# Scores of a neighbourhood-attention mixer: two stacked products over 128 rows, or three split products over 64 rows with two heads on the two halves of the array

## The chip, the core and the metric

The kernel runs on one core of a Trainium2 chip. A core has a matrix engine (TensorE, "PE" in the profile, with its weight loads listed apart as "PEld"), VectorE ("DVE"), ScalarE ("ACT"), GpSimd ("POOL") and a queue engine (SyncE, "SP") that mostly issues DMAs. A matmul keeps one operand in the array (the stationary one, loaded beforehand), streams the other past it, and adds up over the array's rows, which are partitions of on-chip memory. Results go to banks of a separate memory, PSUM, 128 partitions by 512 floats each. The metric is the time of one execution on the device in microseconds; lower is better.

## What is computed

A bidirectional encoder of two layers over 512 tokens of width 1024, in float32. Each layer is a half feed-forward step, a token mixer, a cross-attention into 256 memory tokens and another half feed-forward step, each followed by a layer norm. The change is in the mixer of the odd layer (there is one): neighbourhood attention on a grid of 8 rows by 64 columns, 16 heads of width 64. Each token attends to all 8 rows and 16 neighbouring columns, with a learned bias.

```python
def mixer_c(h, w_in, w_out, rpb):
    q, k, v = jnp.split(h @ w_in, 3, axis=-1)
    ...
    def row_block(r):
        ...
        bias = rpb[:, dr[None, :, None] + NA_KH - 1, dc[:, None, :] + NA_KW - 1]
        s = jnp.einsum('bwhd,bawjhd->bhwaj', q_r, k_nb).astype(jnp.float32) * scale
        s = s + bias.astype(jnp.float32)[None]
        p = jax.nn.softmax(s.reshape(B, C_HEADS, GRID_W, kh * kw), axis=-1)
        p = p.reshape(B, C_HEADS, GRID_W, kh, kw).astype(v.dtype)
        return jnp.einsum('bhwaj,bawjhd->bwhd', p, v_nb)
    ...
    return o @ w_out
```

## The kernel before

Everything is kept transposed where TensorE needs it: features on partitions, 512 tokens along the free axis. To get float32 results from a one-pass format ("fp32r"), each operand is split into a high part and the rest: `split` (L364) rounds on ScalarE and subtracts on VectorE. A product of two split operands is three matmuls: high by high, high by low, low by high (`mm3`, L375).

`mixer_c` (L1247) works on eight pairs of heads. One pair's queries are a 128 by 512 product: the first head's 64 features are on partitions 0 to 63, the second head's on 64 to 127; the same holds for the keys. `queries` (L1270) and `keys` (L1286) project them into a PSUM bank and split them into two small tiles ("t2", 128x512). They then copy halves of these between partitions by DMA on SP's queue. A head's query tile gets its 64 high rows on top and its 64 low rows below; its two key tiles hold the high rows twice and the low rows twice. One matmul over 128 rows then gives (high + low) of the query by one part of the key, and two matmuls give all four products. That takes 4 copies for queries and 8 for keys of each pair, 128 KB each. In the profile they are "slab<-t" on SP's queue.

`weights_of` (L1323) makes the scores. The 64 grid columns are taken in four column blocks (`C_BLOCKS`, L36): 128 queries (16 columns of 8 rows) against 24, 32, 32 and 24 columns of keys, which is 192, 256, 256 and 192 keys. For each of the two heads, one after the other, and each block: two matmuls into a PSUM bank of tag "a"; VectorE adds the bias, writes the sum to a t2 tile and takes the minimum (the scores are negated); ScalarE takes the exponential with its sum. After a head's four blocks, a reciprocal on VectorE and four normalisations on ScalarE follow.

`turned` (L1353) then transposes the weights on TensorE and splits them; `attend` (L1366) multiplies them with the values into two banks of tag "d". `values` (L1253) projects values, `share` (L1386) and `down` (L538) the output.

Nothing is issued in the order in which it is written. All calls go to `Graph.record` (L138). `Graph.plan` (L182) runs a simple model of the engines over the recorded operations, with costs from `Graph.cost` (L113), and fixes each engine's order. On TensorE the ready operation that was recorded first goes first; on VectorE, ScalarE and GpSimd a second pass orders by due time. Buffers of a tag are granted in the order of recording as they come free: 14 for "t2", 27 for "slab" (128x1024), and for PSUM banks 3 for "a", 2 for "d" and 3 for "t" (`BUFS`, L341). The loop of `mixer_c` (L1401) records for each pair: the next pair's keys, the transposes of this pair's weights, the queries after next, the next pair's `weights_of`, this pair's `attend`, then values. Every operation is called from one helper, so the profile puts nearly all of them on L157, and they are told apart by their tiles.

Of the kernel before, what the change touches and what calls it, by code (L numbers as in the profile page):

```python
# [12 lines left out]
F32 = mybir.dt.float32  # L13
# [3 lines left out]
AF = mybir.ActivationFunctionType  # L17
ALU = mybir.AluOpType
AX = mybir.AxisListType

P = 128
# [7 lines left out]
ROWS = S // GRID_W  # L29
# [6 lines left out]
C_BLOCKS = [(0, 24, 0), (8, 32, 1), (24, 32, 1), (40, 24, 2)]  # L36
# [29 lines left out]
class Graph:  # L66
# [45 lines left out]
    @staticmethod  # L112
    def cost(engine, method, out, ins, kw):  # L113
        n = 1
        for d in (out if method != "tensor_reduce" else ins[0]).ap[1:]:
            n *= d[1]
        wide = any(z.space == bass.MemoryType.PSUM for z in ins + [out]) if engine != "sync" else False
        if method == "dma_start":
            return 1200.0 if "accum_op" in kw else 600.0
        if engine == "tensor":  # L120
            return max(n / 2.4 + 14, 111)
        scalars = sum(1 for z in ins if z.ap[-1][1] == 1)
        aside = 120.0 * any(Graph.extent(z)[0] > 0 for z in ins + [out])
        if engine == "vector":
            if method == "tensor_scalar" and not wide:
                n = n / 2
            return n / 0.96 + 72 + aside + 60 * scalars + 120 * (method == "scalar_tensor_tensor" and "accum_out" in kw)
        if engine == "scalar":
            scaled = 42 * hasattr(kw.get("scale"), "tensor")
            return n / 1.2 + (55 if wide else 100) + aside + 45 * scalars + 130 * ("accum_out" in kw) + scaled  # L130
        if n <= 8:
            return 270.0 if method == "tensor_scalar" else 200.0 if method != "tensor_tensor" else 390.0 + 157.0 * n
        if method == "memset":
            return n * 0.83 + 60
        dense = len(ins) == 2 and all(z.ap[-1][0] != 0 for z in ins)
        return n * (2.4 if dense else 1.7) + (70 if dense else 130)
# [184 lines left out]
class Kernel:  # L321
# [925 lines left out]
    def mixer_c(self, ln_i, last):  # L1247
        nc, a = self.nc, self.a
# [21 lines left out]
        def queries(pair, first=False):  # L1270

            if pair % 2 == 0:
                wq[0] = self.w_cols(w_in, 128 * pair)
            ps = self.ps("a" if first else "d")
            for lo, hi in [(0, 128), (128, 256), (256, 512)] if first else [(0, 512)]:
                self.project(wq[0][pair % 2], ps, lo, hi)
            parts = self.t2(), self.t2()
            self.split(ps, *parts, scale=-0.125)
            qs[pair] = self.pair()
            for s, z in enumerate(qs[pair]):  # L1280
                for i, part in enumerate(parts):
                    nc.sync.dma_start(
                        out=z[64 * i : 64 * i + 64].bitcast(F32), in_=part[64 * s : 64 * s + 64].bitcast(F32)
                    )

        def keys(pair, first=False):  # L1286

            if pair % 2 == 0:
                wk[0] = self.w_cols(w_in, D + 128 * pair)
            ps = self.ps("a" if first else "t")  # L1290
            for lo, hi in [(0, 256), (256, 512)] if first else [(0, 512)]:
                self.project(wk[0][pair % 2], ps, lo, hi)
            parts = self.t2(), self.t2()
            self.split(ps, *parts)
            ks[pair] = [self.pair() for _ in range(2)]
            for s, both in enumerate(ks[pair]):
                for z, part in zip(both, parts):
                    for i in range(2):
                        nc.sync.dma_start(
                        out=z[64 * i : 64 * i + 64].bitcast(F32), in_=part[64 * s : 64 * s + 64].bitcast(F32)  # L1300
                    )

        def biases(pair):

            table, inner = self.t2(F32), self.t2(F32)
            got = []
            for s in range(2):
                tab = table[:, s * 256 : s * 256 + 256]
                nc.gpsimd.dma_start(out=tab, in_=self.bias[2 * pair + s])
                outer = self.t2(F32)  # L1310
                dst = [outer[:, 0:192], inner[:, s * 256 : s * 256 + 256], outer[:, 192:384]]
                for i, off in enumerate((64, 0, 0)):
                    n = dst[i].shape[1]
                    nc.gpsimd.tensor_tensor(
                        out=dst[i].rearrange("p (u r) -> p u r", r=8),
                        in0=self.near[:, i, : n // 8].rearrange("p (u o) -> p u o", o=1).broadcast_to([P, n // 8, 8]),
                        in1=tab[:, off : off + n].rearrange("p (u r) -> p u r", r=8),
                        op=ALU.subtract,
                    )
                got.append(dst)  # L1320
            return got

        def weights_of(pair):  # L1323

            got = []
            for q, k, table in zip(qs.pop(pair), ks.pop(pair), biases(pair)):
                both = [self.t2(F32), self.t2(F32)]
                nc.gpsimd.memset(both[0][:, 0:64], 0.0)
                nc.gpsimd.memset(both[1][:, 448:512], 0.0)
                l = self.small(4, "l4")  # L1330
                us = []
                for t, (kc, w, kind) in enumerate(C_BLOCKS):
                    n = w * ROWS
                    ps = self.ps("a")
                    for i in range(2):
                        nc.tensor.matmul(
                            ps[:, :n], q[:, t * P : (t + 1) * P], k[i][:, kc * 8 : kc * 8 + n], start=i == 0, stop=i == 1
                        )
                    c0 = (t % 2) * 256 + (64 if t == 0 else 0)
                    u = both[t // 2][:, c0 : c0 + n]  # L1340
                    mn = self.small(1, "mn")
                    nc.vector.tensor_tensor_reduce(
                        out=u, in0=ps[:, :n], in1=table[kind], scale=1.0, scalar=3e38, op0=ALU.add, op1=ALU.min, accum_out=mn,
                    )
                    nc.scalar.activation(u, u, AF.Exp, bias=mn, scale=-1.0, accum_out=l[:, t : t + 1])
                    us.append(u)
                nc.vector.reciprocal(l, l)
                for t, u in enumerate(us):
                    self.normalise(u, l[:, t : t + 1])
                got.append([z[:, c * 256 : c * 256 + 256] for z in both for c in range(2)])  # L1350
            return got

        def turned(us):  # L1353

# [38 lines left out]
        vp, qs, ks, acts = {}, {}, {}, []  # L1393
        wv, wq, wk, wo = [None], [None], [None], {}
        for t in range(NT):
            values(0, t)
        queries(0, True)
        keys(0, True)
        queries(1)
        us = weights_of(0)  # L1400
        for pair in range(8):  # L1401


            if pair < 7:
                keys(pair + 1)
            else:
                for n in range(3, 5):
                    share(n)
            pts = turned(us)
            if pair < 6:  # L1410
                queries(pair + 2)
            else:
                for n in (0, 1) if pair == 6 else (5, 6, 7):
                    share(n)
            if pair < 7:
                us = weights_of(pair + 1)
            acts.append(attend(pts, pair))
            if pair == 6:
                self.memory_tokens()
            if pair < 6:  # L1420
                for t in range(2):
                    values(pair // 2 + 1, 2 * (pair % 2) + t)
            elif pair == 6:
                share(2)
# [241 lines left out]
```

## Time and profile before

| | |
|---|---|
| time of the kernel, median of 3 runs | 2128.33 us (2128.21 to 2129.47) |
| span of the profiled execution, first to last instruction | 2123.9 us |
| that execution's own whole time | not given; the median lies 4.4 us above the span |
| mean granted TensorE clock | 0.998 |

The profile is of one execution. Times in its lines are microseconds unless marked ns. "a<-slab,slab" reads: written to a tile of tag a, from tiles of tag slab. "128*128 128x256" on a matmul is 128 array rows by 128 columns with an output of 128 partitions by 256. A windows line gives a stretch, its length, then for PE, PEld, DVE, ACT and POOL the busy time with the number of instructions, the granted clock, the share of time of the DMA engines and GB/s. Matmuls are pipelined and the ends in their records are modelled, so the time from one start to the next tells what a matmul takes, not its length.

### The profile page before, as it was taken

The page shows a single profiled execution, that of the slowest core. Times are in us where ns is not written, and L with a number is a line of the kernel's source. Part 1 is how long each engine was busy: PE and PEld are TensorE (multiplying, and loading weights), DVE is VectorE, ACT ScalarE, POOL GpSimd, SP SyncE. Part 2 cuts the span into 40 slices and gives each one's busy share as a digit, 9 for nine tenths or more (in the row PEclk, how much of TensorE's full clock was granted, in tenths as well). Part 3 has the DMA queues.
Part 4 walks back from the last instruction along what each step waited for, and adds up shares of the span by engine and source line. Part 5 has one row for each costly group of instructions (what it writes and reads, how often), then busy time and mean ns, then how long its engine had stood idle before and what let it go on. Part 6 is the DMA issues. An engine that isn't in the chain of part 4 may idle for free.

```text
span 2123.9 us, 32745 instructions
## 1 busy us (share of the span) xinstructions
PE 2109.2 (99%) x12648; PEld 1871.0 (88%) x12648; DVE 1735.8 (82%) x2500; ACT 1161.2 (55%) x1903; POOL 287.4 (14%) x379
## 2 busy tenths in 40 slices
PE   9999999999999999999999999999999999999997
PEld 7999988888888899998889999888888888999996
DVE  7789988888748879998879999866577479699997
ACT  5555443698546554545545455457764465444552
POOL 0001015310102000000200000312210021000003
PEclk9999999999999999999999999999999999999999
DMA  6566562004434346564445556356454433456551
GB/s 205 141 168 144 136 191 91 21 18 116 140 125 109 90 117 181 150 158 129 148 100 143 126 139 186 78 147 165 119 165 155 139 93 96 110 149 155 143 149 60
DMA packets 208860, 275.93 MB, mean 130 GB/s; under 512 B 10688, under 2 KB 151616, under 8 KB 208704
## 3 DMA queue, kind: packets, MB, share of 16 engines
q1 hardware_dynamic: 175904, 221.14, 34.0%
q0 software_dynamic: 32512, 52.44, 14.1%
q8 instruction: 100, 1.64, 0.3%
q14 instruction: 56, 0.46, 0.1%
q10 hardware_dynamic: 288, 0.26, 0.0%
HBM read 259.12 MB, written 4.19 MB: 124 GB/s over the span
## 4 chain that ended last, share of the span: by engine, by line
PE 96%; DVE 1%; ACT 1%; DMA 1%; issue 0%; SPq 0%; DVEq 0%; ACTq 0%
PE a L157 59%; PE d L157 23%; PE t L157 15%; DVE slab L157 1%; ACT t L157 1%; DMA slab<-t 1%; DVE x L157 0%; ACT slab L157 0%; SPq L157 0%; DVE t L157 0%; DMA raw<-x_t 0%; ACT xh L157 0%; DVE mn L157 0%; DVE xl L157 0%; DVEq L1662 0%
## 5 line engine op out<-in xcount | busy, mean ns | idle before, releaser
L157 DVE TENSOR_TENSOR slab<-slab,slab 128x1024 fp32r<-128x1024 f32 (+3 forms) x638 | 727.5, 1166 | 69.5 <-ACT slab L157 39.9
L157 ACT CAST slab<-slab 128x1024 fp32r<-128x1024 f32 (+2 forms) x498 | 472.7, 983 | 341.5 <-DVE slab L157 173.2
L157 PE MATMUL a<-slab,slab 128*128 128x256 f32 (+3 forms) x2320 | 567.2, 322 | 0.7 <-DMA slab<-t 0.4
L157 PE MATMUL a<-xh,slab 128*128 128x256 f32 (+2 forms) x2480 | 559.9, 315 | 0.3 <-ACT slab L157 0.3
L157 PE MATMUL d<-slab,slab 128*128 128x512 f32 (+2 forms) x1856 | 447.0, 381 | 0.0
L157 PEld LDWEIGHTS a<-xh,slab 128*128 128x128 f32 x2480 | 416.4, 190 | 33.7 <-ACT slab L157 1.0
L157 PEld LDWEIGHTS a<-slab,slab 128*128 128x128 f32 x2320 | 409.5, 190 | 38.8 <-ACT t L157 1.3
L157 PE MATMUL a<-xl,slab 128*128 128x256 f32 (+1 forms) x1240 | 389.7, 314 | 0.0
L157 PE MATMUL a<-raw,slab 128*128 128x256 f32 x2048 | 388.9, 283 | 0.1
L157 PEld LDWEIGHTS d<-slab,slab 128*128 128x128 f32 x1856 | 329.0, 189 | 55.9 <-issue 0.2
L157 PEld LDWEIGHTS a<-raw,slab 128*128 128x128 f32 x2048 | 327.9, 192 | 5.4 <-ACT slab L157 0.5
L157 PEld LDWEIGHTS a<-xl,slab 128*128 128x128 f32 x1240 | 236.0, 190 | 18.4 <-DVE xl L157 0.4
L157 PE MATMUL t<-slab,slab 128*128 128x512 f32 (+1 forms) x840 | 209.5, 389 | 0.0
L157 DVE TENSOR_TENSOR slab<-raw,slab 128x1024 fp32r<-128x1024 f32 (+2 forms) x140 | 160.2, 1160 | 18.6 <-ACT slab L157 18.4
L157 PEld LDWEIGHTS t<-slab,slab 128*128 128x128 f32 x840 | 149.9, 189 | 26.3
L157 DVE TENSOR_TENSOR slab<-t,slab 128x512 fp32r<-128x512 f32 (+2 forms) x223 | 137.6, 638 | 16.4 <-ACT slab L157 15.9
L157 ACT CAST slab<-t 128x512 fp32r<-128x512 f32 (+2 forms) x223 | 120.9, 566 | 40.7 <-DVE t L157 13.9
L157 ACT CAST slab<-raw 128x1024 fp32r<-128x1024 f32 (+1 forms) x132 | 124.3, 971 | 27.9 <-PE a L157 8.8
L157 DVE SCALAR_TENSOR_TENSOR x<-d,x 128x512 f32<-128x512 f32 x168 | 114.7, 685 | 25.3 <-PE d L157 24.4
L157 ACT COPY t<-a 128x512 f32<-128x512 f32 (+1 forms) x116 | 63.5, 550 | 130.4 <-PE a L157 77.2
L157 POOL DMA_DIRECT2D slab<-ffn_w_down x40 | 47.7, 1193 | 310.3 <-DVE slab L157 276.3
L157 ACT ACTIVATE t<-a 128x512 f32<-128x512 f32 (+3 forms) x65 | 36.3, 559 | 89.0 <-PE a L157 89.0
(126 smaller groups left out, 2167.2 us busy)
## 6 DMA issues: line engine op xcount, KB each, us to landing
slab<-ffn_w_gate SPq DMA_DIRECT2D x80, 512.0 KB
slab<-ffn_w_up SPq DMA_DIRECT2D x80, 512.0 KB
slab<-ffn_w_down SPq DMA_DIRECT2D x80, 512.0 KB
slab<-ffn_w_down POOLq DMA_DIRECT2D x40, 512.0 KB, 5.8
raw<-mem_w_kv SPq DMA_DIRECT2D x16, 1024.0 KB
slab<-t SPq DMA_DIRECT2D x96, 128.0 KB
slab<-ffn_w_gate POOLq DMA_DIRECT2D x16, 512.0 KB, 7.8
slab<-ffn_w_up POOLq DMA_DIRECT2D x16, 512.0 KB, 6.0
```

What stands on the lines that cost most here:

```text
L157: op.call = lambda: fn(*args, **kw)
```

## The change

- The copies between partitions are gone. `queries` and `keys` split the projected bank straight into one pair of slabs (`split_t2`, L948: ScalarE writes the high part, VectorE the rest); both heads stay where the projection put them.
- A head's score block is now three matmuls over the 64 rows on which the head lies: high by high, high by low, low by high. The product low by low, which the stacked form added, is left out.
- The two heads of a pair are made together: for each column block two "a" banks are asked for, and the six matmuls are recorded alternating between the heads, so between the upper and the lower 64 rows of the array.
- Bias, minimum and exponential follow for both heads of a block; the reciprocals and normalisations come after the last block of both heads.
- In the planner's costs, a matmul with a 64-row operand or output counts half, and one with plain float32 operands four passes.

```diff
         if engine == "tensor":
-            return max(n / 2.4 + 14, 111)
+            passes = 4 if method == "matmul" and ins[0].dtype == F32 else 1
+            beside = 2 if ins[0].shape[0] == 64 or out.shape[0] == 64 else 1
+            return max(n * passes / 2.4 + 14, 111) / beside
...
-            parts = self.t2(), self.t2()
-            self.split(ps, *parts, scale=-0.125)
-            qs[pair] = self.pair()
-            for s, z in enumerate(qs[pair]):
-                for i, part in enumerate(parts):
-                    nc.sync.dma_start(
-                        out=z[64 * i : 64 * i + 64].bitcast(F32), in_=part[64 * s : 64 * s + 64].bitcast(F32)
-                    )
+            qs[pair] = self.split_t2(ps, scale=-0.125)
...
-            parts = self.t2(), self.t2()
-            self.split(ps, *parts)
-            ks[pair] = [self.pair() for _ in range(2)]
-            for s, both in enumerate(ks[pair]):
-                for z, part in zip(both, parts):
-                    for i in range(2):
-                        nc.sync.dma_start(
-                        out=z[64 * i : 64 * i + 64].bitcast(F32), in_=part[64 * s : 64 * s + 64].bitcast(F32)
-                    )
+            ks[pair] = self.split_t2(ps)
...
-            got = []
-            for q, k, table in zip(qs.pop(pair), ks.pop(pair), biases(pair)):
-                both = [self.t2(F32), self.t2(F32)]
...
-                for t, (kc, w, kind) in enumerate(C_BLOCKS):
-                    n = w * ROWS
-                    ps = self.ps("a")
-                    for i in range(2):
+            tables, q, k = biases(pair), qs.pop(pair), ks.pop(pair)
+            both = [[self.t2(F32), self.t2(F32)] for _ in range(2)]
...
+            for t, (kc, w, kind) in enumerate(C_BLOCKS):
+                n = w * ROWS
+                ps = [self.ps("a") for _ in range(2)]
+                for i, (x, y) in enumerate(((0, 0), (0, 1), (1, 0))):
+                    for s in range(2):
+                        own = slice(64 * s, 64 * s + 64)
                         nc.tensor.matmul(
-                            ps[:, :n], q[:, t * P : (t + 1) * P], k[i][:, kc * 8 : kc * 8 + n], start=i == 0, stop=i == 1
+                            ps[s][:, :n], q[x][own, t * P : (t + 1) * P], k[y][own, kc * 8 : kc * 8 + n], start=i == 0, stop=i == 2
                         )
...
-                    nc.scalar.activation(u, u, AF.Exp, bias=mn, scale=-1.0, accum_out=l[:, t : t + 1])
-                    us.append(u)
+                    nc.scalar.activation(u, u, AF.Exp, bias=mn, scale=-1.0, accum_out=sums[s][:, t : t + 1])
+                    us[s].append(u)
+            for l, u4 in zip(sums, us):
                 nc.vector.reciprocal(l, l)
-                for t, u in enumerate(us):
+                for t, u in enumerate(u4):
                     self.normalise(u, l[:, t : t + 1])
...
```

More of the change, by code (lines that the diff above doesn't have):

```diff
@@ L1323, in weights_of @@
         def weights_of(pair):
-            got = []
-            for q, k, table in zip(qs.pop(pair), ks.pop(pair), biases(pair)):
-                both = [self.t2(F32), self.t2(F32)]
[L1328 to L1331, printed above, removed]
-                for t, (kc, w, kind) in enumerate(C_BLOCKS):
-                    n = w * ROWS
-                    ps = self.ps("a")
-                    for i in range(2):
+            tables, q, k = biases(pair), qs.pop(pair), ks.pop(pair)
@@ new lines, in weights_of @@
+            both = [[self.t2(F32), self.t2(F32)] for _ in range(2)]
+            sums = [self.small(4, "l4") for _ in range(2)]
+            us = [[], []]
+            for z in both:
+                nc.gpsimd.memset(z[0][:, 0:64], 0.0)
+                nc.gpsimd.memset(z[1][:, 448:512], 0.0)
+            for t, (kc, w, kind) in enumerate(C_BLOCKS):
[4 more added lines that the diff above has]
+                        own = slice(64 * s, 64 * s + 64)
@@ L1336, in weights_of @@
                         nc.tensor.matmul(
-                            ps[:, :n], q[:, t * P : (t + 1) * P], k[i][:, kc * 8 : kc * 8 + n], start=i == 0, stop=i == 1
+                            ps[s][:, :n], q[x][own, t * P : (t + 1) * P], k[y][own, kc * 8 : kc * 8 + n], start=i == 0, stop=i == 2
                         )
-                    c0 = (t % 2) * 256 + (64 if t == 0 else 0)
-                    u = both[t // 2][:, c0 : c0 + n]
+                c0 = (t % 2) * 256 + (64 if t == 0 else 0)
@@ L1341, in weights_of @@
+                for s in range(2):
+                    u = both[s][t // 2][:, c0 : c0 + n]
                     mn = self.small(1, "mn")
                     nc.vector.tensor_tensor_reduce(
-                        out=u, in0=ps[:, :n], in1=table[kind], scale=1.0, scalar=3e38, op0=ALU.add, op1=ALU.min, accum_out=mn,
+                        out=u, in0=ps[s][:, :n], in1=tables[s][kind], scale=1.0, scalar=3e38, op0=ALU.add, op1=ALU.min, accum_out=mn,
                     )
-                    nc.scalar.activation(u, u, AF.Exp, bias=mn, scale=-1.0, accum_out=l[:, t : t + 1])
@@ L1346, in weights_of @@
-                    us.append(u)
+                    nc.scalar.activation(u, u, AF.Exp, bias=mn, scale=-1.0, accum_out=sums[s][:, t : t + 1])
+                    us[s].append(u)
+            for l, u4 in zip(sums, us):
                 nc.vector.reciprocal(l, l)
-                for t, u in enumerate(us):
+                for t, u in enumerate(u4):
                     self.normalise(u, l[:, t : t + 1])
-                got.append([z[:, c * 256 : c * 256 + 256] for z in both for c in range(2)])
@@ L1351, in weights_of @@
-            return got
+            return [[z[:, c * 256 : c * 256 + 256] for z in pair for c in range(2)] for pair in both]
         def turned(us):
```

## The prediction

> **What bounds the kernel now.** I read the page first: the engines' busy shares and the chain that ended last.
>
> ```profile
> span 2123.9 us, 32745 instructions
> ...
> PE 2109.2 (99%) x12648; PEld 1871.0 (88%) x12648; DVE 1735.8 (82%) x2500; ACT 1161.2 (55%) x1903; POOL 287.4 (14%) x379
> ...
> PE 96%; DVE 1%; ACT 1%; DMA 1%; issue 0%; SPq 0%; DVEq 0%; ACTq 0%
> ```
>
> TensorE is never long idle, and 96% of the chain is its own work. A busy PE may still hide stalls, since matmul records overlap, so I asked for the stretch of the odd mixer from its first score to its last (windows view), and for three of the eight stretches in which one pair's scores are made.
>
> ```profile
> 1418.70:1573.00 154.30, 153.81 (x881) 132.71 (x881) 96.40 (x255) 113.44 (x289) 36.26 (x82) 1.00 0.59 156
> ...
> 1455.94:1459.48 3.54, 3.33 (x26) 3.05 (x25) 2.58 (x14) 3.24 (x9) 2.19 (x4) 1.00 0.55 135
> 1501.10:1504.37 3.27, 3.27 (x27) 3.06 (x25) 2.61 (x14) 2.72 (x10) 1.28 (x3) 1.00 0.48 117
> 1545.91:1549.33 3.42, 3.33 (x26) 3.03 (x25) 2.67 (x14) 2.68 (x9) 1.74 (x4) 1.00 0.62 151
> ```
>
> In 154.30 us PE is busy 153.81 at a granted clock of 1.00, while VectorE (96.40), ScalarE (113.44) and POOL have room and the DMA share is 0.59. So the mixer lasts as long as the matmuls stand in line. The change is worth what it does to that line; whatever it takes off the other engines, SP's queue or the DMAs counts only where PE waits for it.
>
> The price of one place in the line comes from the start times, not from the durations. This is PE's timeline for the third pair (start, length, then the work; a row merges neighbours and shows the first's shape, so the x6 are two of 192 columns and four of 256):
>
> ```profile
> 1455.94 0.88 PE L157 MATMUL a<-slab,slab 128*128 128x192 f32 x6
> 1456.65 0.28 PE L157 MATMUL d<-slab,slab 128*128 128x256 f32 x1
> 1456.86 0.47 PE L157 MATMUL a<-slab,slab 128*128 128x192 f32 x2
> 1457.16 0.30 PE L157 MATMUL d<-slab,slab 128*128 128x256 f32 x1
> 1457.30 0.26 PE L157 MATMUL a<-slab,slab 128*128 128x192 f32 x1
> 1457.78 0.33 PE L157 MATMUL a<-slab,slab 128*128 128x192 f32 x1 [0.21 <-DMA slab<-t]
> 1457.94 0.90 PE L157 MATMUL d<-slab,slab 128*128 128x256 f32 x6
> 1458.67 0.40 PE L157 MATMUL a<-slab,slab 128*128 128x256 f32 x2
> 1458.91 0.28 PE L157 MATMUL d<-slab,slab 128*128 128x256 f32 x1
> 1459.03 0.61 PE L157 MATMUL a<-slab,slab 128*128 128x256 f32 x4
> 1459.48 1.02 PE L157 MATMUL d<-slab,slab 128*128 128x256 f32 x7
> 1460.33 0.40 PE L157 MATMUL t<-slab,xh 128*128 128x512 f32 x1
> ```
>
> Seven of 256 columns start from 1459.48 to 1460.33: 0.121 each, so **0.120 us a place**. Narrower ones are held by their weight loads, seen where the columns are 128 (timeline of the loads):
>
> ```profile
> 1400.07 0.30 PEld L157 LDWEIGHTS a<-xh,slab 128*128 128x128 f32 x2
> 1400.30 0.19 PEld L157 LDWEIGHTS a<-xl,slab 128*128 128x128 f32 x1
> 1400.41 0.30 PEld L157 LDWEIGHTS a<-xh,slab 128*128 128x128 f32 x2
> ```
>
> Three loads in 0.34 us: **0.112 us** is the least between two, and I take it for 192 columns.
>
> **The change part by part.** *Score products.* The groups of that stretch give the count:
>
> ```profile
> L157 PE MATMUL d<-slab,slab 128*128 128x256 f32 x112 | 19.9, 286 | 0.0
> ...
> L157 PE MATMUL a<-slab,slab 128*128 128x192 f32 x64 | 14.0, 278 | 0.5 <-DMA slab<-t 0.4
> L157 PE MATMUL a<-slab,slab 128*128 128x256 f32 x64 | 12.9, 293 | 0.0
> ```
>
> Before: 64 × 0.112 + 64 × 0.120 = 14.8 us. After: three products for two, 96 + 96 = 192, each with its own load. If each takes a place, that is 22.3 us: **+7.4**. No instruction here uses 64 rows, so whether two halves run side by side isn't shown. Bounds for a block (one column block, both heads): six places if they don't, against four now (+0.23 us); three if they do (−0.12 us). The nearest rows, the loads above, never start closer than 0.112 us, so I take six and keep three for the range.
>
> *The order.* Even if halves can overlap, they must be neighbours. Score banks are "a", and there are three (L341). A block now takes two. With all three free the first block of a pair gets both banks and alternates its heads; the third bank admits the first head of the next block alone. Then VectorE frees one bank at a time (timeline of VectorE):
>
> ```profile
> 1457.67 0.41 DVE L157 CUSTOM_DVE_ANT_0 t<-a,t 128x256 f32<-128x256 f32 x1
> ...
> 1458.01 0.35 DVE L157 CUSTOM_DVE_ANT_0 t<-a,t 128x192 f32<-128x192 f32 x1
> ```
>
> They stand 0.34 apart. The plan counts a triple at three times 111 ns halved, about 0.17, and gives PE the earliest recorded work that is ready; attention products or values, ready in all of the fences above, fill each gap. So I expect per pair one run of nine products, then five lone triples: six groups. One block in four is paired at best. The added wait, for a block's second bank, stands in PE's fixed order: behind it the attention products and values queue, and behind those VectorE's bank copies; where the bank comes later than planned, all of them are late.
>
> *The copies.* Their issues, and SP's row ahead of the third pair:
>
> ```profile
> slab<-t SPq DMA_DIRECT2D x96, 128.0 KB
> ```
>
> ```profile
> 1449.43 9.72 SPq L157 DMA_DIRECT2D slab<-t  x12
> ```
>
> All 96 go (12.6 MB), with SP's time for them. Twelve copies are in the queue until 1459.15, while scores begin at 1455.94; the row at 1457.78 names this wait. What is PE's loss? The third pair's stretch holds 16 scores and 9 products of 256: 0.90 + 0.96 + 1.08 = 2.94 us of 3.54, so 0.60 lost. The other two stretches above also hold 25 loads: 0.33 and 0.48. Mean 0.47, times eight: **3.8 us** of stall at most, part for copies and part for banks. Bank waits shrink too where three products pass per bank instead of two, but SP's earlier weight loads may start other work on VectorE. I take half, **−1.9**, bounds −3.8 and 0.
>
> *Beside PE.* The two split instructions per projection stay, at the same size, into other buffers: nothing. Four t2 buffers and one slab fewer per pair: earlier bias tables and weights, for which PE doesn't wait. Each head's reciprocal and normalisation now come after both heads' last block: eight normalisations at
>
> ```profile
> L157 ACT ACTIVATE t<-t,l 128x256 f32<-128x256 f32 x80 | 36.6, 501 | 0.5 <-DVE l L157 0.5
> ```
>
> are 4.0 us at most. The next pair's keys hide them (24 places of 512 columns, over 5 us), and behind the last pair
>
> ```profile
> 1573.03 8.35 PE L157 MATMUL a<-slab,slab 128*128 128x512 f32 x36
> ```
>
> does; without cover they would cost up to 4 us a pair. Costs in the planner: no other instruction has 64 rows, so the order ahead of the mixer stays.
>
> **Sum:** +7.4 − 1.9 = +5.5. The profiled span is 2123.9; its own whole time isn't given, the median 2128.33 lies 4.4 above it, and I carry that unchanged: 2123.9 + 5.5 + 4.4 = **2133.8**. With the stall's bounds alone: 2131.9 to 2135.7.
>
> **The rivals.** *1. The halves overlap, but only in paired blocks.* A paired block saves 0.348 against two lone triples. Eight of 32: 7.4 − 8 × 0.348 − 1.9 = +2.7, **2131.1** (2129.2 to 2133). For: the two heads use other rows and other banks. Against: nothing in the trace runs two matmuls at once. [...]
>
> *2. Going between 64 and 128 rows costs something.* Six groups a pair have 96 borders. Where PE must empty itself, the hidden end of a matmul shows: 286 ns (group row) less the place of 120 is 0.166 us, 15.9 in all: +21.4, **2149.7**; at half of it 2141.7. Against: going to transposes and back is free:
>
> ```profile
> 1448.63 1.03 PE L157 MATMUL t<-ident,t 128*128 128x128 f32 x8
> 1449.42 0.48 PE L157 MATMUL d<-xh,slab 128*128 128x512 f32 x1
> 1449.73 0.40 PE L157 MATMUL d<-xl,slab 128*128 128x512 f32 x1
> ```
>
> Eight transposes and the first product take 1.10 us, about what eight loads and a 512-column place come to. But those keep 128 rows. [...]
>
> *3. Faster: halves overlap and most blocks are paired.* With p paired blocks the change is 7.4 − 0.348 p − 1.9: even at p = 16, faster by 0.2% from p = 28; all 32 give −5.6, **2122.7**. It needs VectorE to free two banks before PE picks again, which the 0.34 us apart speak against.
>
> *4. The copies were hidden and the order alone decides*, with nothing measurable: 2128.
>
> **How the numbers follow.** Forecast 0.36, rival 1 0.26, rival 2 0.28, rival 3 0.06, rival 4 0.04. A measurement tells some 0.2% (4.3 us) from no change: 2124.1 to 2132.6. Slower than that: 0.30 of the forecast, 0.03 of rival 1, all of rival 2, 0.01 of rival 4: 0.62. Same: 0.06, 0.23, 0.02 of rival 3, 0.02 of rival 4: 0.33. Faster: 0.05. The range runs from 2127, below rival 1 with its whole stall gained, to 2150, rival 2 at full price; outside lie rival 3 and an exposed weight load on top of rival 2.
>
> **What would show it.** PE's timeline: groups of nine and three score products per pair, and their start distances. About 0.11 to 0.12 between alternating halves confirms the forecast; 0.06 on average, rival 1. Distances over 0.2 us at the borders of a group show rival 2. Runs of six alternating halves at most blocks show rival 3. No "DMA slab<-t" may end a wait, and the score stretches should lose under 0.3 us each. The forecast is wrong if a lone triple costs clearly other than 0.34 to 0.36 us, or if PE's line outside the scores grows.

## The result, and the profile after

| | before | after |
|---|---|---|
| median of 4 runs each | 2128.27 us | 2149.46 us (2147.3 to 2154.95) |
| ratio | | 1.0104, 95% interval 1.0092 to 1.0117 |
| span of the profiled execution | 2123.9 us | 2147.7 us |

The changed kernel is slower by 21.2 us, where 5.5 was forecast. The page, busy shares and chain:

```profile
span 2147.7 us, 32564 instructions
...
PE 2133.1 (99%) x12712; PEld 1881.9 (88%) x12712; DVE 1739.6 (81%) x2500; ACT 1161.8 (54%) x1903; POOL 289.8 (13%) x379
...
PE 98%; DVE 1%; ACT 1%; issue 0%; DMA 0%; DVEq 0%; ACTq 0%
```

Nothing here says what is wrong. PE has 64 more matmuls and 23.9 us more of busy time, the other engines are as they were, and the DMA's part of the chain now rounds to 0%. The windows view of the mixer, from its first score product to its last, shows where the time is:

```profile
1419.70:1594.50 174.80, 174.79 (x940) 141.38 (x939) 97.85 (x251) 114.17 (x288) 33.17 (x74) 0.99 0.22 72
```

The stretch shown before, 154.30 us, ran to 1573.00, which is 0.9 us past its last score. From the first score's start to the last one's end, 153.35 us (1418.75 to 1572.10) have become 174.85 (1419.73 to 1594.58): 21.5 of the 23.8 us between the spans. Another 1.0 us had passed before the first score, over matmuls whose order is the same in both kernels. The stretch now starts 939 matmuls instead of 871 (64 more of the scores, four more of other work); their 68 places come to 7.9 us, over a third of it. The DMA share fell from 0.59 to 0.22, which bought nothing. The granted clock, 1.00 before, is 0.99. PE's timeline shows the rest. These are the last pair's scores (start, length, then the work):

```profile
1589.46 0.61 PE L159 MATMUL a<-slab,slab 64*128 64x256 f32 x3
1590.00 0.38 PE L159 MATMUL d<-slab,slab 128*128 128x256 f32 x1
1590.32 0.62 PE L159 MATMUL a<-slab,slab 64*128 64x256 f32 x3
1590.86 0.38 PE L159 MATMUL d<-slab,slab 128*128 128x256 f32 x1
1591.18 0.61 PE L159 MATMUL a<-slab,slab 64*128 64x256 f32 x3
1591.72 0.38 PE L159 MATMUL d<-slab,slab 128*128 128x256 f32 x1
```

The order is as forecast: lone triples of one head with one attention product between them. But from one attention product to the next it takes 0.86 us (1590.00 to 1590.86) where four places of 0.12 would be 0.48. And the triple is not what is dear: the attention product, 128 rows and 256 columns as before, holds the line for 0.32 us instead of 0.12, and the triple for 0.54 instead of 0.36. The weight loads at the same time say why:

```profile
1589.46 0.41 PEld L159 LDWEIGHTS a<-slab,slab 64*128 64x128 f32 x3
1590.00 0.19 PEld L159 LDWEIGHTS d<-slab,slab 128*128 128x128 f32 x1
1590.32 0.41 PEld L159 LDWEIGHTS a<-slab,slab 64*128 64x128 f32 x3
1590.86 0.19 PEld L159 LDWEIGHTS d<-slab,slab 128*128 128x128 f32 x1
```

Where the rows change from 64 to 128 or back, the load starts together with its own matmul (1590.00 in both views, 1590.32 in both). At all 96 borders of the mixer the two starts are at most 3 ns apart. So at each border the load lies open, where in e1_full_rows, the same order without borders, the loads start 0.11 and 0.12 us ahead (shown below); the rows show the late start, not its cause.

For the sums below I added up, for every matmul from the first score to the last, the time from its start to the next start, less its place: 0.227 us for 512 columns, 0.120 for 256, 0.112 for 192, 0.109 for a transpose (the medians of these distances in that stretch of the kernel before are 0.227, 0.119, 0.113 and 0.109). Before, this surplus was 4.2 us, which is the stall; after, it is 17.6. The 48 groups of 64-row products (seven of nine, two of six, 39 of three) each carry some 0.38 us of it where a group stands clear of the next.

### The profile page after: what moved, and what is told of

It reads as the page before. It is cut to its first block, busy times and chain, and to the rows that moved or that the text cites. A ratio compares the mean times of both kernels' runs of the same rounds, so it can differ in the third digit from the quotient of the medians.

```text
span 2147.7 us, 32564 instructions
## 1 busy us (share of the span) xinstructions
PE 2133.1 (99%) x12712; PEld 1881.9 (88%) x12712; DVE 1739.6 (81%) x2500; ACT 1161.8 (54%) x1903; POOL 289.8 (13%) x379
## 4 chain that ended last, share of the span: by engine, by line
PE 98%; DVE 1%; ACT 1%; issue 0%; DMA 0%; DVEq 0%; ACTq 0%
PE a L159 59%; PE d L159 24%; PE t L159 15%; DVE x L159 0%; DVE slab L159 0%; ACT slab L159 0%; ACT t L159 0%; DMA raw<-x_t 0%; DVE t L159 0%; DVE xl L159 0%; ACT xh L159 0%; DVE mn L159 0%; DVEq L1652 0%; DVE l L159 0%; DVE nmu L159 0%
## 5 line engine op out<-in xcount | busy, mean ns | idle before, releaser
L159 PE MATMUL a<-slab,slab 128*128 128x256 f32 (+4 forms) x2384 | 576.3, 323 | 0.2
L159 PE MATMUL d<-slab,slab 128*128 128x512 f32 (+2 forms) x1856 | 453.0, 384 | 0.0
L159 PEld LDWEIGHTS a<-slab,slab 128*128 128x128 f32 (+1 forms) x2384 | 412.9, 190 | 44.6 <-issue 3.8
L159 PEld LDWEIGHTS a<-xl,slab 128*128 128x128 f32 x1240 | 236.4, 191 | 18.2
L159 DVE TENSOR_TENSOR slab<-t,slab 128x512 fp32r<-128x512 f32 (+2 forms) x230 | 142.3, 641 | 23.2 <-ACT slab L159 22.6
L159 ACT ACTIVATE t<-a 128x512 f32<-128x512 f32 (+2 forms) x64 | 35.7, 558 | 87.5 <-PE a L159 87.5
```

The source lines that it names most:

```text
L159: op.call = lambda: fn(*args, **kw)
```

## The experiments

Two theories were set against each other. *Borders*: each group of 64-row products costs about 0.37 us for going in and out, whatever is in it. *Waits*: borders are free; the time goes to three products per bank, to lone triples and to what waits behind them in this order. Every run is compared with the kernel before that ran beside it. Runs e1 and e2 come from two rounds, and the kernel before was 2.4 us faster in the second, so single microseconds are compared within a round or in the traces.

| run | groups of 64-row products | median, us | before beside it | ratio (95%) |
|---|---|---|---|---|
| changed kernel | 48 | 2149.46 | 2128.27 | 1.0104 (1.0092 to 1.0117) |
| e1_full_rows | 0 | 2131.40 | 2127.84 | 1.0019 (1.0009 to 1.0028) |
| e1_pairs | 31 | 2132.42 | 2127.84 | 1.0021 (1.0011 to 1.0031) |
| e1_two_blocks | 16 | 2125.73 | 2127.84 | 0.9991 (0.9982 to 1.0000) |
| e1_no_copies_alone | none | 2130.52 | 2127.84 | 1.0013 (1.0003 to 1.0022) |
| e2_plain_costs | 23 | 2137.46 | 2125.41 | 1.0054 (1.0039 to 1.0069) |
| e2_two_blocks_full | 0 | 2131.14 | 2125.41 | 1.0024 (1.0015 to 1.0034) |
| e2_one_group | 8 | 2123.85 | 2125.41 | 0.9990 (0.9980 to 0.9999) |
| e2_copies_left_out | none | 2126.36 | 2125.41 | 1.0002 (0.9992 to 1.0011) |
| e3_one_group | 8 | 2122.74 | 2127.29 | 0.9980 (0.9972 to 0.9989) |
| e3_two_blocks | 16 | 2125.77 | 2127.29 | 0.9993 (0.9984 to 1.0002) |
| e3_stacked_two_blocks | none | 2130.23 | 2127.29 | 1.0013 (1.0004 to 1.0022) |
| e3_changed_again | 48 | 2152.03 | 2127.29 | 1.0112 (1.0099 to 1.0126) |

### The same order without borders: e1_full_rows

```diff
-    ps[s][:, :n], q[x][own, t * P : (t + 1) * P], k[y][own, kc * 8 : kc * 8 + n], ...
+    ps[s][:, :n], q[x][:, t * P : (t + 1) * P], k[y][:, kc * 8 : kc * 8 + n], ...
+    nc.ops[-1].ns /= 2
```

> The changed kernel with its order kept, but each score product takes all 128 rows of queries and keys, so each score sums both heads of the pair (that part of the computation is changed). No 64-row matmul is left, so no border between row modes. Border theory (each of the 48 groups of 64-row products costs about 0.37 us for going in and out): 2149.5 - 48 x 0.37 + 9 paired blocks that no longer overlap x 0.35 = 2134.8. Rival (the borders are free; the time goes to the third product per bank and the waits behind it in this order): order and count are the same, so it stays at 2147 or more.

2131.40, 18 us less, with every matmul in the same place of the line; the rival is out. The same pattern as above, in PE's timeline of this run:

```profile
1438.22 0.28 PE L159 MATMUL d<-slab,slab 128*128 128x256 f32 x1
1438.34 0.52 PE L159 MATMUL a<-slab,slab 128*128 128x256 f32 x3
1438.70 0.29 PE L159 MATMUL d<-slab,slab 128*128 128x256 f32 x1
```

One attention product and a triple now take 0.48 us (1438.22 to 1438.70) instead of 0.86: the 0.38 is the price of a group, two borders, 0.19 each. The loads of this run (timeline of the weight loads) stand ahead of their matmuls again, 1438.23 for the triple at 1438.34 and 1438.58 for the product at 1438.70:

```profile
1438.23 0.42 PEld L159 LDWEIGHTS a<-slab,slab 128*128 128x128 f32 x3
1438.58 0.19 PEld L159 LDWEIGHTS d<-slab,slab 128*128 128x128 f32 x1
```

The run is 3.6 us above the kernel before: 64 more places are +7.4, and the surplus in the stretch fell from 4.2 to 1.5, −2.7, which leaves +4.7, an error of 1.1. The expectation was 3.4 higher; it started from the changed kernel's time, which held 2.6 us of half clock as well (below).

### All blocks alternating: e1_pairs

```diff
+    nc.tiles[ps[1 - s].tensor.name]["users"].add(nc.ops[-1])
```

> The changed kernel, but a block's products wait for both of its banks, so all 32 blocks alternate their heads, in 31 groups instead of 48. Border theory: 23 more paired blocks x 0.35 and 17 fewer groups x 0.37 off 2149.5: 2135.2. Rival (borders free): 32 blocks x 0.345 = 11 us of score places against 14.8 before, so 2126 or less.

2132.42, 2.8 below the border theory's number for the same reason, and above the kernel before although its score places are 11.1 us against 14.8; the rival is out here too. The borders outweigh what the pairing gains.

### Two column blocks in a bank: e1_two_blocks, e3_two_blocks

```diff
-            for t, (kc, w, kind) in enumerate(C_BLOCKS):
-                n = w * ROWS
-                ps = [self.ps("a") for _ in range(2)]
+            for g in range(2):
+                ps = [self.ps("a") for _ in range(2)]
+                blocks = [(t, *C_BLOCKS[t]) for t in (2 * g, 2 * g + 1)]
+                for t, kc, w, kind in blocks:
+                    n, at = w * ROWS, t % 2 * 256
...
+                            ps[s][:, at : at + n], q[x][own, t * P : (t + 1) * P], k[y][own, kc * 8 : kc * 8 + n],
```

> The changed kernel with two column blocks of a head in one bank and both heads' banks asked for together: 16 groups of 12 alternating products. Border theory: 2149.5 - 23 x 0.35 - 32 x 0.37 = 2129.6, within 1.5 of the kernel before. Rival (borders free): as in e1_pairs, 2126 or less.

> e1_two_blocks again, beside e3_one_group on one chip: 1.5 to 2.5 us below the kernel before. If its first gain was chance: level with it.

The same products, all alternating, in 16 groups: 2.1 and 1.5 us below the kernel before, both at the edge of the noise (the intervals reach 1.0000 and 1.0002). By its number alone, 2125.73, this run would also fit the rival; the border theory's figure is 3.9 too high, 2.6 of it the half clock. It is e1_full_rows and e1_pairs that exclude the rival. Against e1_pairs, 15 groups fewer are worth 6.7 us; 0.9 of that is a wait for VectorE inside one group of e1_pairs (at 1579.95), and the rest is 0.39 each, the border price. Two of the groups in PE's timeline:

```profile
1434.00 0.96 PE L159 MATMUL a<-slab,slab 64*128 64x192 f32 x12
1434.89 1.81 PE L159 MATMUL d<-slab,slab 128*128 128x256 f32 x13
1436.63 0.94 PE L159 MATMUL a<-slab,slab 64*128 64x256 f32 x12
1437.49 0.63 PE L159 MATMUL d<-slab,slab 128*128 128x256 f32 x3
```

Twelve products in 0.89 and 0.86 us, the border included: 0.07 each.

### What alternating halves are worth: e2_two_blocks_full

```diff
-    ps[s][:, at : at + n], q[x][own, t * P : (t + 1) * P], k[y][own, kc * 8 : kc * 8 + n],
+    ps[s][:, at : at + n], q[x][:, t * P : (t + 1) * P], k[y][:, kc * 8 : kc * 8 + n],
```

> e1_two_blocks over all 128 rows, in the same order: each score sums both heads of the pair (that part of the computation is changed). Neither borders nor halves side by side. If halves that alternate overlap fully and a group costs 0.38: 2125.7 - 16 x 0.38 + 32 x 0.348 = 2130.8. If alternating halves gain nothing: 2125.7 - 6.1 = 2119.6.

2131.14, and 2119.6 is out. The terms give 11.1 − 6.1 = 5.0 us against e1_two_blocks. Between the spans of the two profiled executions (2128.6 and 2123.8) stand 4.8 us, and between their stretches from the first score's start to the last one's 5.4 (1418.75 to 1576.55 against 1419.12 to 1571.55). Compared by the kernel before of each round the difference would be 7.8, since that of the second round was 2.4 faster. Two halves side by side take one place. The timeline of e3_one_group below shows it directly, 0.12 us from one pair of 256 columns to the next, since there the two heads' banks have different tags.

### One group per pair: e2_one_group, e3_one_group

```diff
-            for g in range(2):
-                ps = [self.ps("a") for _ in range(2)]
+            banks = [self.ps(tag) for tag in "aaat"]
...
+                        for z in banks:
+                            nc.tiles[z.tensor.name]["users"].add(nc.ops[-1])
```

> e1_two_blocks taken further: a pair's eight score blocks in four banks (three of tag a, one of tag t), asked for together, so one group of 24 alternating products per pair, 8 in all. Border theory: 2125.7 - 8 x 0.38 = 2122.7. Rival (the transposes and keys miss the fourth bank, or VectorE gets eight blocks at once and is late): 2126 or more.

> e2_one_group again beside e3_two_blocks on one chip. 8 groups against 16 at 0.38: 3.0 us below e3_two_blocks and 4 to 5 below the kernel before. If the fourth bank is missed elsewhere: level with e3_two_blocks.

The first try gave 1.6 us and couldn't be told from the two-block version of another round; its profiled execution lost 2 us in the first 30 us of the program (the 101st matmul starts at 28.44, before at 26.33), ahead of anything that was edited. Beside it on one chip it is 3.0 us below the two-block version, as eight groups at 0.38 say, and **4.6 us below the kernel before: 0.9980 (0.9972 to 0.9989)**, faster than both kernels of this case. In its timeline the two halves start in the same hundredth:

```profile
1434.26 0.28 PE L159 MATMUL a<-slab,slab 64*128 64x256 f32 x1
1434.26 0.28 PE L159 MATMUL t<-slab,slab 64*128 64x256 f32 x1
1434.38 0.28 PE L159 MATMUL a<-slab,slab 64*128 64x256 f32 x1
1434.38 0.28 PE L159 MATMUL t<-slab,slab 64*128 64x256 f32 x1
1434.50 0.25 PE L159 MATMUL a<-slab,slab 64*128 64x192 f32 x1
1434.50 0.25 PE L159 MATMUL t<-slab,slab 64*128 64x192 f32 x1
```

### The planner's price undone: e2_plain_costs

```diff
-            return max(n * passes / 2.4 + 14, 111) / beside
+            return max(n / 2.4 + 14, 111)
```

> The changed kernel with one part undone: the planner prices a 64-row product like any other, as before. Its fixed order then has 23 groups instead of 48 (per pair nine, twelve, three). If the price sits in the borders and the halved cost is what cut the groups up: from e1_full_rows 2131.4 + 23 x 0.38 - 8 paired blocks x 0.35 - some 3 for heads that overlap where triples meet = 2134. Rival (the number of lone triples and banks decides, not the order): 2147 or more.

12.1 us above the kernel before instead of 21.2: the halved price in the planner is itself a cause of 9 of them, some 2.6 of these through the half clock, of which this run has none (its mean granted clock is 0.998). (The edited line also takes back the four passes; PE's first 8578 matmuls, up to the first scores, stand in the same order with either line.) The second pair in PE's timeline has a group of nine and one of twelve:

```profile
1437.22 0.95 PE L159 MATMUL a<-slab,slab 64*128 64x192 f32 x9
1438.11 0.38 PE L159 MATMUL d<-slab,slab 128*128 128x256 f32 x1
1438.42 1.72 PE L159 MATMUL a<-slab,slab 64*128 64x256 f32 x12
1440.07 0.85 PE L159 MATMUL d<-slab,slab 128*128 128x256 f32 x5
```

How the price does it I read from the planner's code. With the halved price, the plan thinks a triple is over in 0.17 us, sees VectorE free the next bank later than that, and puts other work in between: a border each way. At the full price the next bank is free when the triple ends, and triples join up to groups of twelve. The expectation was too low: +6.5 against its own chip by its terms, +12.1 measured. The surplus of the stretch is 7.4 us; without the borders (23 × 0.38 = 8.7) and with the overlaps counted from the starts (42 places, 4.9 us) 3.6 are left, where e1_full_rows has 1.5. So 2.1 us are waits that came back, for banks inside the longer groups among them, and 0.9 are overlaps that I had counted too many. Of the other 2.6, this profile had lost 2.0 before its first score (1420.78 against 1418.75), where PE's order is unchanged; that may be this execution's own, and I can't place it in the median.

### The copies: e2_copies_left_out, e1_no_copies_alone

```diff
-            ks[pair] = [self.pair() for _ in range(2)]
-            for s, both in enumerate(ks[pair]):
-                for z, part in zip(both, parts):
-                    for i in range(2):
-                        nc.sync.dma_start(
...
+            ks[pair] = [self.split_t2(ps)] * 2
```

> The kernel before with its two products over 128 rows, but the copies are left out and nothing takes their place: the products read the unshifted halves, so the scores are not the reference's (low rows of the query are not used, and both heads are summed). Copies worth the three named waits: 2126.9. Worth all stall of the score stretches: 2124. Hidden: 2127.8.

In this run the first head reads the pair's high query part and the second its low part. No gain that can be measured: 1.0002 (0.9992 to 1.0011). The trace names waits for copies, and with them gone the surplus of the stretch is 3.2 us instead of 4.2: 1 us at most, which the whole time doesn't show. The other way to be rid of them:

```diff
+            for s, (hi, lo) in enumerate(ks[pair]):
+                for o in (s, 1 - s):
+                    nc.scalar.copy(hi[own(o)], ps[own(s)])
...
+                    nc.vector.tensor_tensor(out=lo[own(o)], in0=ps[own(s)], in1=hi[own(s)].bitcast(F32), op=ALU.subtract)
```

> One part alone: the kernel before with its stacked two products over 128 rows, but ScalarE and VectorE write the halves into place (8 more small instructions a pair) and the 96 copies are gone. If the copies cost only the three waits that the trace names (0.36, 0.27, 0.32): about 2127.3. If all stall of the score stretches (3.8 us at most) was theirs: 2124.5. If they were hidden: 2128.3.

Slower by 2.7 us, which none of the three cases had. The windows view of its score stretch:

```profile
1418.70:1577.00 158.30, 155.51 (x881) 132.71 (x880) 115.27 (x281) 130.27 (x320) 31.03 (x74) 1.00 0.23 74
```

The same 881 matmuls, but VectorE went from 96.40 us to 115.27 and ScalarE from 113.44 to 130.27, and PE now waits for them (158.30 for 155.51 busy). The copies were the cheaper way.

### Fewer banks, no 64 rows: e3_stacked_two_blocks

```diff
-                    ps = self.ps("a")
+                for g in range(2):
+                    ps = self.ps("a")
+                    blocks = [(t, t % 2 * 256, *C_BLOCKS[t]) for t in (2 * g, 2 * g + 1)]
```

> The kernel before, copies and two products over 128 rows kept; only two column blocks of a head share one bank, so PE waits for banks less often. No 64-row product. If the stall of the score stretches is for banks: 2 to 3 us below the kernel before. If the order takes it back: level with it.

A miss: 2.9 us slower than the kernel before, with a surplus of 6.9 us in the stretch. So the gain of e3_one_group is not that of fuller banks alone. Here the trace puts 2.5 us of PE's idle time down to copies (four waits ended by "DMA slab<-t", the longest 1.0 us), against 0.4 in the kernel before (two waits). That is most of the 2.7 by which the surplus grew; that the copies are the cause was not tested in this order.

### The clock: e3_changed_again

No edit.

> The changed kernel once more, for its clock. If the half-clock stretches of 3.4 us come from PE doing too little in the strings of lone triples, they again stand right behind such strings, and each costs about 1.5 us, so an execution with n of them has a span of about 2144.6 + 1.5 n. If they come by chance, they stand elsewhere too.

The first profile of the changed kernel had two stretches of 3.4 us at half clock in the mixer (its clock records have them from 1443.906 to 1447.319 and from 1594.092 to 1597.506), this one four, at 1443.5, 1494.7, 1545.9 and 1597.1; no other run has one before its end (mean granted clocks of 0.998 and 0.999, against 0.997 and 0.995 in these two). The windows view, first the stretch of lone triples ahead of a drop in the first profile and the drop itself, then the four drops of this run:

```profile
1440.30:1443.80 3.50, 3.50 (x19) 2.61 (x19) 1.69 (x9) 1.23 (x5) 0.15 (x1) 1.00 0.30 99
1443.90:1447.30 3.40, 3.40 (x12) 2.90 (x12) 0.74 (x4) 1.57 (x5) 0.00 (x0) 0.50 0.00 0
```

```profile
1443.50:1446.90 3.40, 3.40 (x12) 2.92 (x13) 1.02 (x4) 1.85 (x7) 0.00 (x0) 0.50 0.00 0
1494.70:1498.10 3.40, 3.40 (x13) 2.92 (x12) 1.85 (x5) 1.81 (x6) 0.00 (x0) 0.50 0.09 23
1545.90:1549.30 3.40, 3.40 (x13) 2.94 (x14) 2.17 (x7) 2.29 (x7) 0.00 (x0) 0.50 0.00 0
1597.10:1600.50 3.40, 3.40 (x12) 2.86 (x12) 1.74 (x5) 3.36 (x14) 0.00 (x0) 0.50 0.21 28
```

All six stand right behind a string of lone triples: in the 3.6 us ahead of each, PE ran 17 to 19 matmuls, 12 or 13 of them of 64 rows, with seven or eight borders. The spans are 2147.7 with two drops and 2150.3 with four: 1.3 us each, near the 1.5 expected. Strings in other pairs passed without one. The starts of the drops give a hint: here they stand 51.2 us apart each time and in the first profile 150.2, which is 15 and 44 times one and the same 3.413 us, the recorded length of both drops of the first profile. Its stretches of full clock up to the first drop, between the two and behind the second, 1437.011, 146.773 and 542.719 us, are 421, 43 and 159 such lengths. So in each of the two executions the drops start on a fixed grid in time. Divided along this grid, the mixer of the first profile has seven borders in two of the stretches, 1440.49 to 1443.91 and 1590.68 to 1594.09, the two ahead of its drops, and at most six in any other. So a string seems to bring a drop only where it fills the stretch that ends at a point of the grid; that is my estimate from this one execution. What such a stretch must hold stays open: in the first profile the one from 1385.88 to 1389.29, 16 lengths ahead of the first drop, has PE busy for only 2.59 of its 3.41 us, without 64-row products, and no drop followed, while in the two ahead of the drops the busy column shows no idle time at all (3.41 of 3.41 us).

## Why the prediction was wrong

It had the direction and the place, and its range held the time (2149.46, at the upper end of 2150), but the likeliest case had a quarter of the size. By its steps:

- **The bound.** Right. Nearly all of the change is in PE's line within the mixer (21.5 of 23.8 us from the first score to the last, and 1.3 for a drop of the clock right behind); 12.6 MB less of DMA traffic and SP's free queue moved nothing.
- **The order.** Right in six of the eight pairs (nine, then five lone triples), and in all, by luck, in the total: 48 groups and 96 borders. The first pair has five groups, the last seven.
- **The places.** The size was off for paired blocks. I took one weight load at a time, since no two in the rows that I had read started closer than 0.112 us. Loads to different halves do overlap (in the changed kernel's nine paired blocks the loads of the two heads start 2 to 10 ns apart; in e3_one_group the matmuls of both heads start at 1434.26), and two halves share a place (rival 1). With this order only 9 of 32 blocks profit: 9 × 0.348 = 3.1 us less than my +7.4.
- **The border: the step that failed.** The forecast took going between 64 and 128 rows at nothing, since going to transposes and back is free (eight and a product in 1.10 us, as their places come to). That row was the wrong neighbour: a transpose uses all 128 rows (128*128 in its row). The sign put down for rival 2, distances over 0.2 us at the borders, came: a lone triple takes 0.54 us and the attention product beside it 0.32. The bound from the hidden end of a matmul, 0.166 us a border, was near what e1_full_rows shows, 0.19; that PE empties itself there is not shown. 48 × 0.38 = 18.2 us. The other groupings agree (0.39 a group between e1_pairs and e1_two_blocks, 0.38 between e3_two_blocks and e3_one_group), and e1_full_rows, the same order without them, is 18 us faster.
- **The stall.** −1.9 was taken, −2.7 came (4.2 to 1.5 in e1_full_rows). In the old order the copies are worth 1.0 us of stall at most (e2_copies_left_out); what gave the rest isn't shown.
- **Not in it at all:** the clock, 2 × 1.3 = 2.6 us in the profiled execution, and the planner's halved price as the maker of the many groups. I used that price to forecast the order, and didn't ask what the old one would have given.

The sum with the measured sizes: 7.4 − 3.1 + 18.2 + 2.6 − 2.7 = +22.4 against 23.8 between the two spans; 1.0 of the rest lies ahead of the first score. Rival 2's 2149.7 was hit, but partly by luck: the overlap that it left out and the clock that nobody had cancel.

## What to carry to other kernels

Two 64-row matmuls side by side took one place in this kernel (0.12 us for 256 columns), but each return trip from 128 rows cost 0.38 us, about what three places of 256 columns cost: count the groups that the order will have, not the products, and make the groups long (here 24 products in one, by sharing banks and asking for all of them at once). A planner that is told a cheaper price for an instruction may spread it out; look at the order that it makes, not only at the price. A copy that the trace names as the end of a wait isn't a cost until its removal is timed, in the order that it is about.

## What was not expected of the hardware

- In the changed kernel no weight load starts ahead across a border between 64 and 128 rows: at all 96 of them load and matmul start within 3 ns of each other, and a 128-row product between two triples holds the line for 0.32 us instead of 0.12.
- In the mixer the granted clock fell to 0.50 for 3.4 us at a time (3.413 in the first profile) though PE is recorded busy for all 3.41 us ahead of both drops of the first profile, only behind strings of lone 64-row triples (six of six drops) and, in the two executions that show it, at distances of 15 and 44 times 3.413 us (51.2 and 150.2).
